# A sparse expert layer whose last tiles reach the residual by a one-hot product, and the two mixers behind it

## The chip, the cores and the metric

The kernel runs on one core of a Trainium2 chip, in one launch. The metric is the device time in microseconds (us) of that core; the time before is the median of three runs. A core has TensorE (PE in the rows; PEld is its weight load), VectorE (DVE), ScalarE (ACT), GpSimd (POOL) and SyncE (SP, which here issues most DMAs). All tensors are float32.

## The reference, cut to what matters

Two transformer-like blocks over 512 tokens of width 1024. The part around the change is the second half of each layer of the first block, a mixture of 16 experts of which each token takes two, and the mixer that follows it.

```python
x = x + g1 * mixer_i(rmsnorm(x, mix_norm[i]) * (1 + sc1) + sh1)     # layer 0: fox, layer 1: MLA
h = rmsnorm(x, ffn_norm[i]) * (1 + sc2) + sh2
# hier_moe: a group of 4 experts by softmax, 2 experts in the group, weights in `combine` (T x 16)
a = einsum('td,edf->tef', h, w_gate); u = einsum('td,edf->tef', h, w_up)      # d 1024, f 256
out = einsum('tef,efd->td', silu(a) * u * combine[..., None], w_down)
x = x + g2 * out                                   # g2: a row of 1024 from the conditioning
...
# second block, after layer 1: 16 meta rows ahead of the tokens (528), then
h = rmsnorm_2(concat(meta, x), norm_pre[0])
u = h @ w_in + b_in                                # 1024 -> 8192: x0, x1, v, z, 2048 channels each
y = bidir_long_conv(dwconv(v) * dwconv(x1), filters) * dwconv(x0) * silu(z)  # the hyena mixer
```

## The kernel before, in words

Tokens lie in four tiles of 128 rows (`NT`), and the residual `self.x` stays on the chip in four tiles of 128x1024. A float32 product is three matmuls (`mm3`, L147) of a rounded part and a rest: `split` (L121) makes the rounded part on ScalarE (L125) and the rest on VectorE (L128). `weights` (L136) loads a block of 512 KB into a `raw` buffer (L133, a ring of 8 in the expert phase) and splits it.

`moe(l)` sorts the tokens by expert into tables of 128 row numbers per expert (`tix` as integers, `tf` as floats, with the weights beside them) and goes over 16 experts. `front(e)` (L1174) gathers an expert's rows and computes its gate and up products (`expert_in`, L1021); `expert_out` (L1044) transposes the result, splits it, multiplies by the down weights into two PSUM banks (12 matmuls of 512 columns), has ScalarE copy these to `yo` (one buffer, L1060) and GpSimd add `yo` row by row to the array `yd` in DRAM (an indirect DMA, L1061). `front(e+1)` is issued ahead of `expert_out(e)`, so that down product e stands behind gate and up product e+1 on TensorE. Between them lie parts of the filters that the hyena mixer needs later (`hy_filter`, a generator: 32 parts a layer, of which 30 in layer 0 and 28 in layer 1 are spread over the loop).

An expert with more than 128 tokens leaves the rest to overflow tiles, numbered in `otab`. The weights of the first are loaded whether it exists or not, with the expert's number in a register (six blocks); `tc.If(n_any > 0)` (L1206) holds its work, and `tc.For_i(1, n_ov, 1)` (L1209) goes over further ones. With these inputs layer 0 has none and layer 1 has one: 16 scatters in layer 0 and 17 in layer 1, and neither layer goes round the loop. Behind it stand the last filter parts (two in layer 0, four in layer 1).

The next phase reads `yd` back (`moe_sum`, L1220 to L1222): four tiles of 512 KB by SyncE. `moe_norm` (L338) multiplies a tile by the gate row `g2` (L346, L359), adds it to the residual (L345), sums the squares (VectorE for tile 0, L354; ScalarE for others, L352), takes the root on GpSimd (L119), scales (L360), in layer 0 adds a shift (L362), and transposes the tile on TensorE (`put_T`, L374), a tile after the other.

In `mla` (L704) the projection 1024 to 672 follows, as two halves of 336 columns: `gemm_tok` does the first half of all four token tiles, then the second half of all (L774 copies the results), with the weights of the first half asked for between the reads of the sums. In `hyena` (L1389) the tokens of 528 columns are cut into two halves of 264, so that the first half needs token tiles 0 and 1 only; `streams(ct)` (L1465) computes the four projections of a channel tile one after the other, both halves each, and there are 16 channel tiles.

SyncE's queue, and each engine's order, are those in which the program issues its instructions.

Of the kernel before, what the change touches and what calls it, by code (L numbers as in the profile page):

```python
# [10 lines left out]
F32 = mybir.dt.float32  # L11
F32R = mybir.dt.float32r
BF16 = mybir.dt.bfloat16
I32 = mybir.dt.int32
# [58 lines left out]
class Model:  # L73
# [264 lines left out]
    def moe_norm(self, ys, gain, hT, c0, tags, shift=None):  # L338


        nc, ph = self.nc, self.ph
        V = nc.vector

        def add(t):
            return V.tensor_add(self.x[t], self.x[t], ys[t])  # L345
        V.tensor_mul(ys[0], ys[0], self.g2)  # L346
        add(0)
        for t in range(NT):
            x, h = self.x[t], ys[t]
            ss, r = [self.sm.tile([128, 1], F32, tag=n, name=n) for n in ("ss", "rstd")]  # L350
            if t:
                nc.scalar.activation(h, x, AF.Square, accum_out=ss)  # L352
            else:
                V.tensor_tensor_reduce(out=h, in0=x, in1=x, op0=ALU.mult, op1=ALU.add, scale=1.0, scalar=0.0, accum_out=ss)  # L354
            self.rsqrt(r, ss, 1.0 / D, EPS)
            if t < 2:
                self.midpow = self.lastpow
            if t < NT - 1:
                V.tensor_mul(ys[t + 1], ys[t + 1], self.g2)  # L359
            m = V.scalar_tensor_tensor(h, x, r, gain, op0=ALU.mult, op1=ALU.mult)  # L360
            if shift is not None:
                m = V.tensor_add(h, h, shift)  # L362
            if t < NT - 1:
                self.order(add(t + 1), m)
            self.put_T(h, hT, c0 + t * 128, tags)
            yield t
# [337 lines left out]
    def mla(self):  # L704
# [3 lines left out]
        with Phase(self, "mla", dict(mm=2, pv=1, sc=2, tq=2, tp=1), bufs,  # L708
# [7 lines left out]
            ys = [ph.t([128, D], F32, "qT", "y") for _ in range(NT)]  # L716
            sh, A = [ph.t([128, D], F32, "v", n) for n in ("sh", "A")]
            self.moe_sum(0, 0, ys[0])
            self.mod_to(A, 1, 1)
            self.mod_to(sh, 1, 0)  # L720
            self.moe_sum(0, 1, ys[1])
            raws = [self.raw(w_in(0)(0), 672)]
            self.moe_sum(0, 2, ys[2])
            raws.append(self.raw(w_in(0)(1), 672))
            self.moe_sum(0, 3, ys[3])
            raws.append(self.raw(w_in(0)(2), 672))
            h4 = four()
            for t in self.moe_norm(ys, A, h4, 0, ("tq", "tp"), sh):
                if t == 0:
                    pre = [self.weights(z, 672, keep=True) for z in raws + [w_in(0)(3)]]  # L730
            self.dump("xm0", self.x)
            hT = [[z[k // 4][:, k % 4, :] for k in range(KD)] for z in h4]
# [33 lines left out]
            ct = {}  # L766

            def evac_in(c):
                def f(t, p):
                    if c == 0:  # L770
                        if t % 2 == 0:
                            ct[t] = ph.t([128, 2, 672], F32, "PT", "ct")
                            ct[t], ct[t + 1] = ct[t][:, 0, :], ct[t][:, 1, :]
                    nc.scalar.copy(ct[t][:, c * 336:(c + 1) * 336], p)  # L774
                return f
            for c in range(2):
                self.gemm_tok(hT, KD, w_in(c), 336, evac_in(c), pre=None if c else pre)
# [266 lines left out]
    def expert_out(self, th, dn_w, idx, yd):  # L1044
# [19 lines left out]
    def moe(self, l):  # L1064
# [4 lines left out]
        with Phase(self, f"moe{l}", dict(dn=2, fl=2, mm=2, tp=2), bufs,  # L1069
# [109 lines left out]
            along, have = 32 - (2, 4)[l], 0  # L1179
            front(0)  # L1180
            for e in range(16):
# [8 lines left out]
                while have < (2 * e + 1) * along // 32:  # L1190
                    next(fil, None)
                    have += 1
                dw = lambda b: self.weights(dn[e, b], after=None if e else self.routed)
                self.expert_out(th.pop(e), dw, tix[:, e:e + 1], yd)
                while have < (2 * e + 2) * along // 32:
                    next(fil, None)
                    have += 1
            self.g2 = self.gate(l, 5)

            e = nc.values_load(otab[0:1, 0:1], min_val=0, max_val=15)  # L1200
# [5 lines left out]
            with tc.If(n_any > 0):  # L1206
                tv = self.expert_in(xg, lambda b: self.weights(wg[b]), tf[:, 16, 1:2])
                self.expert_out(tv, lambda b: self.weights(wd[b]), tix[:, 16:17], yd)
            with tc.For_i(1, n_ov, 1) as i:  # L1209
                e = nc.values_load(otab[0:1, ds(i, 1)], min_val=0, max_val=15)  # L1210
                ri = ph.t([128, 2], F32, "ri")
                nc.sync.dma_start(ri, tabd[:, ds(i + 16, 1), :].rearrange("p o n -> p (o n)"))
                rx = ph.t([128, 1], I32, "rx")
                V.tensor_copy(rx, ri[:, 0:1])
                tv = self.expert_in(gather(rx), lambda b: self.weights(dyn(gu, b, e)), ri[:, 1:2])
                self.expert_out(tv, lambda b: self.weights(dyn(dn, b, e)), rx, yd)
            for _ in fil:
                pass

# [897 lines left out]
```

## Time and profile before

| | us |
|---|---|
| median of three runs | 2632.34 |
| lowest and highest | 2628.58, 2633.38 |
| the profiled execution's own time | 2630.58 |
| its span, first to last instruction | 2628.8 |
| TensorE busy in the span | 2368.2 (90%) |
| VectorE busy | 1883.2 (72%) |
| ScalarE busy | 1484.7 (56%) |
| mean granted TensorE clock | 0.953 of full |

Times in the rows are counted from the span's start. A row of the order of time gives its start, its duration, the engine, the line and operation, what it writes and reads, and in brackets how long the engine had been idle before it and what ended that. The ends of matmuls are modelled, so the distance of two starts is a matmul's time in a row of them.

### The profile page before, as it was taken

To read this page: it belongs to the slowest core of one execution; us is meant where nothing else is said; L and a number is where in the kernel's file an instruction comes from. 1 tells how busy PE (TensorE), PEld (TensorE's weight loads), DVE (VectorE), ACT (ScalarE), POOL (GpSimd) and SP (SyncE) were. 2 spreads that over 40 slices of the span, in tenths; PEclk is the share of its full clock that TensorE was granted. 3 is DMA by queue.
4 is the path that set the end of the run, shared out by engine and by line. 5 is a ranking of instruction groups with operands and counts; after the bars stand their busy time and mean duration, and the time that the engine had idled before them with its cause. 6 is when DMAs were issued, how large, how long until landed. Compare 5 with 4: busy or idle time off the path is not lost.

```text
span 2628.8 us, 39566 instructions
## 1 busy us (share of the span) xinstructions
PE 2368.2 (90%) x14551; PEld 1956.1 (74%) x14551; DVE 1883.2 (72%) x4015; ACT 1484.7 (56%) x2902; POOL 258.4 (10%) x268
## 2 busy tenths in 40 slices
PE   6889977997899958895999999999799999999888
PEld 5667756775766746674999999997577777777666
DVE  7888877986688677785566666664657878777755
ACT  5575756885567356783444444443336666665652
POOL 1100113121122022211000000000100000000000
PEclk9899988998999979997999999999899999999989
DMA  7786659997211299995422222224322111112232
GB/s 260 245 256 201 225 165 299 338 314 227 74 34 49 84 287 297 304 289 169 130 94 91 90 90 90 90 68 135 117 96 69 41 73 60 70 52 69 90 108 80
DMA packets 130845, 389.07 MB, mean 148 GB/s; under 512 B 23290, under 2 KB 34794, under 8 KB 129880
## 3 DMA queue, kind: packets, MB, share of 16 engines
q1 hardware_dynamic: 115640, 330.31, 36.9%
q0 software_dynamic: 12704, 47.48, 7.4%
q10 hardware_dynamic: 2304, 8.72, 0.8%
q8 instruction: 116, 1.90, 0.3%
q14 instruction: 81, 0.66, 0.1%
HBM read 332.68 MB, written 53.77 MB: 147 GB/s over the span
## 4 chain that ended last, share of the span: by engine, by line
PE 44%; DVE 5%; ACT 2%; issue 2%; DMA 1%; POOL 0%; POOLq 0%; SPq 0%; ACTq 0%; DVEq 0%
PE ps_mm L150 10%; PE ps_mm L151 10%; PE ps_mm L152 10%; PE ps_sc L1781 1%; PE ps_b L152 1%; PE ps_b L150 1%; PE ps_b L151 1%; PE ps_sc L1782 1%; PE ps_tp L1811 1%; ACT whi L125 1%; PE ps_tl L1723 1%; PE ps_tp L1524 1%; PE ps_pv L150 1%; DVE wlo L128 1%; DMA yd<-yo,tix 1%
## 5 line engine op out<-in xcount | busy, mean ns | idle before, releaser
L128 DVE TENSOR_TENSOR wlo<-raw,whi 128x1024 fp32r<-128x1024 f32 (+3 forms) x426 | 499.9, 1185 | 236.5 <-ACT whi L125 228.6
L125 ACT CAST whi<-raw 128x1024 fp32r<-128x1024 f32 (+3 forms) x426 | 431.4, 1023 | 244.9 <-PE ps_mm L152 84.1
L150 PE MATMUL ps_mm<-hT,whi 128*128 128x264 f32 x1024 | 294.6, 288 | 0.9 <-ACT hT L125 0.8
L151 PE MATMUL ps_mm<-hT,whi 128*128 128x264 f32 x1024 | 293.3, 287 | 0.7 <-DVE hT L128 0.7
L152 PE MATMUL ps_mm<-hT,wlo 128*128 128x264 f32 x1024 | 291.8, 285 | 0.0
L150 PE MATMUL ps_mm<-whi,hT 128*128 128x512 f32 x512 | 206.4, 405 | 6.9 <-DVE zg L1716 5.9
L151 PE MATMUL ps_mm<-wlo,hT 128*128 128x512 f32 x512 | 205.5, 403 | 0.0
L152 PE MATMUL ps_mm<-whi,hT 128*128 128x512 f32 x512 | 205.1, 402 | 0.0
L151 PEld LDWEIGHTS ps_mm<-hT,whi 128*128 128x128 f32 x1024 | 194.7, 190 | 1.1 <-DVE hT L128 1.1
L150 PEld LDWEIGHTS ps_mm<-hT,whi 128*128 128x128 f32 x1024 | 193.9, 189 | 1.6 <-ACT hT L125 1.6
L152 PEld LDWEIGHTS ps_mm<-hT,wlo 128*128 128x128 f32 x1024 | 194.2, 190 | 0.0
L151 PE MATMUL ps_mm<-wlo,un 128*128 128x384 f32 (+1 forms) x376 | 141.2, 377 | 8.0 <-DVE wlo L128 7.7
L150 PE MATMUL ps_mm<-whi,un 128*128 128x384 f32 (+1 forms) x376 | 141.6, 380 | 4.7 <-ACT whi L125 1.6
L152 PE MATMUL ps_mm<-whi,un 128*128 128x384 f32 (+1 forms) x376 | 139.9, 377 | 0.0
L1789 ACT ACTIVATE P<-P,nm 128x528 f32<-128x528 f32 x128 | 94.3, 737 | 70.6 <-DVE P L1786 69.0
L1458 ACT ACTIVATE u<-ps_mm,hb 128x264 f32<-128x264 f32 x96 | 46.3, 482 | 137.5 <-PE ps_mm L152 137.5
L119 POOL TENSOR_TENSOR r<-rs,mhalf 128x4 f32<-128x4 f32 (+1 forms) x72 | 77.8, 1084 | 401.8 <-DVE rs L118 383.4
L150 PEld LDWEIGHTS ps_mm<-whi,hT 128*128 128x128 f32 x512 | 96.7, 189 | 27.3 <-DVE zg L1716 6.8
L150 PE MATMUL ps_mm<-whi,xgT 128*128 128x512 f32 x264 | 108.9, 413 | 7.0 <-ACT xgT L125 7.0
L219 DVE CUSTOM_DVE_ANT_0 ada<-ada,crow 128x1024 f32<-128x1024 f32 x80 | 97.6, 1220 | 19.5 <-DMA ada<-in_w_ada_dram 19.0
L152 PEld LDWEIGHTS ps_mm<-whi,hT 128*128 128x128 f32 x512 | 96.8, 189 | 18.1
L151 PEld LDWEIGHTS ps_mm<-wlo,hT 128*128 128x128 f32 x512 | 96.5, 189 | 17.5 <-issue 0.2
(586 smaller groups left out, 6310.2 us busy)
## 6 DMA issues: line engine op xcount, KB each, us to landing
raw<-in_moe_gu_dram SPq DMA_DIRECT2D x136, 512.0 KB, 7.5
ada<-in_w_ada_dram SPq DMA_DIRECT2D x96, 512.0 KB, 4.2
raw<-in_moe_dn_dram SPq DMA_DIRECT2D x68, 512.0 KB, 6.2
raw<-in_hy_w_dram SPq DMA_DIRECT2D x64, 512.0 KB, 3.5
raw<-in_da_w_dram SPq DMA_DIRECT2D x64, 512.0 KB, 4.9
raw<-in_fox_w_dram SPq DMA_DIRECT2D x32, 384.0 KB, 4.4
hs<-ht ACTq DMA_DIRECT2D x16, 532.0 KB, 7.3
H<-hs SPq DMA_DIRECT2D x16, 532.0 KB, 3.5
```

What stands on the lines that cost most here:

```text
L119: self.lastpow = nc.gpsimd.tensor_tensor(out, t, self.mhalf[:in_.shape[0]].to_broadcast(list(in_.shape)), op=ALU.pow)
L125: nc.scalar.copy(hi, src)
L128: return nc.vector.tensor_sub(lo, src, hi.bitcast(F32))
L150: r = nc.tensor.matmul(o, a[0], b[0], start=first, stop=False)
L151: nc.tensor.matmul(o, a[0], b[1], start=False, stop=False)
L152: self.lastmm = nc.tensor.matmul(o, a[1], b[0], start=False, stop=last)
L219: nc.vector.tensor_tensor_reduce(out=t, in0=t, in1=self.crow, op0=ALU.mult, op1=ALU.add, scale=1.0, scalar=0.0, accum_out=v[:, j:j + 1])
L1458: A.activation(u[:, 1 + hs.start:1 + hs.stop], p, AF.Identity, bias=hb[:, c:c + 1])
L1524: nc.tensor.transpose(p[:, cs], ab[:, f, cs], self.ident)
L1723: nc.tensor.matmul(tp[32 * j:32 * j + 16, 0:64], xt[:, k, :], w[:, c0 + j * 64:c0 + (j + 1) * 64], start=(k == 0), stop=(k == KD - 1))
L1781: nc.tensor.matmul(sc[:, hf, 0:264], qs[mp][:, ts], kk[mp][:, fs], start=True, stop=False)
L1789: nc.scalar.activation(P, P, AF.Exp, bias=nm_, scale=-1.0, accum_out=sum_)
```

## The change

The scatter stays for experts 0 to 14. For expert 15, for the overflow tile and for further tiles `expert_out` gets the row numbers as floats (`tok`): it compares a table 0 to 511 with them, which gives a 128x512 matrix with a one at each row's token, multiplies the down product by `g2` on the way out of PSUM, and multiplies the transposed one-hot matrix with it, in plain float32 and per token tile and half, with VectorE adding each product to the residual. The loop over further tiles stands under a second branch. `out(14)` now precedes `front(15)`; expert 15's down product comes last, after the branches. The sums of `yd` are read, gated and added to the residual in the expert phase, ahead of expert 15's down product, into buffers of the `raw` ring; the filter's remaining parts come after all that (one more is put in front by `fill(31)`).

`moe_norm` loses gate and residual; the gain is multiplied before the root is there, and the shift goes into one instruction with the scale. In `mla` all eight weight blocks are asked for and split ahead of the norm (those of the second half into buffers of the tag `qk`), and the projection goes by token tile, both halves of a tile together. In `hyena` the first channel tile does the first halves of all four projections after token tiles 0 and 1, then the rest of the norm, then the second halves.

```diff
-    def moe_norm(self, ys, gain, hT, c0, tags, shift=None):
+    def moe_norm(self, hs, junk, gain, hT, c0, tags, shift=None):
...
+        def begin(t):
+            ss, rs[t] = [self.sm.tile([128, 1], F32, tag=n, name=n) for n in ("ss", "rstd")]
+            nc.scalar.activation(junk(), self.x[t], AF.Square, accum_out=ss)
+            V.tensor_mul(hs[t], self.x[t], gain)
+            self.rsqrt(rs[t], ss, 1.0 / D, EPS)
             if t < 2:
                 self.midpow = self.lastpow
+        begin(0)
+        for t in range(NT):
+            h, r = hs[t], rs.pop(t)
+            if shift is None:
+                V.tensor_scalar(h, h, r, None, op0=ALU.mult)
+            else:
+                V.scalar_tensor_tensor(h, h, r, shift, op0=ALU.mult, op1=ALU.add)
             if t < NT - 1:
...
+                begin(t + 1)
             self.put_T(h, hT, c0 + t * 128, tags)
             yield t
...
+            ws = [[], []]
+            for b in range(4):
+                w = self.weights(w_in(0)(b), 672)
+                ws[0] += [[z[:, j * 336:(j + 1) * 336] for z in w] for j in range(2)]
+            for b in range(4):
+                raw = self.raw(w_in(1)(b), 672)
+                for j in range(2):
+                    w = [ph.t([128, 336], F32R, "qk", "w1") for _ in range(2)]
+                    self.split(*w, raw[:, j * 336:(j + 1) * 336])
+                    ws[1].append(w)
             h4 = four()
...
+            for t in self.moe_norm(hs, lambda: jk, A, h4, 0, ("tq", "tp"), sh):
+                for c in range(2):
+                    p = ph.bank("mm")[:, :336]
+                    for k in range(KD):
+                        self.mm3(p, [z[k][:, t * 128:t * 128 + 128] for z in hT], ws[c][k], k == 0, k == KD - 1)
+                    nc.scalar.copy(ct[t][:, c * 336:(c + 1) * 336], p)
...
-            for c in range(2):
-                self.gemm_tok(hT, KD, w_in(c), 336, evac_in(c), pre=None if c else pre)
...
-    def expert_out(self, th, dn_w, idx, yd):
+    def expert_out(self, th, dn_w, idx, yd, tok=None):
...
+        if tok is not None:
+            Q = ph.t([128, S], F32, "sel")
+            nc.vector.tensor_scalar(Q, self.iota512, tok, None, op0=ALU.is_equal)
+            for c in range(2):
+                cs = slice(c * 512, (c + 1) * 512)
+                nc.vector.tensor_mul(yo[:, cs], acc[c], self.g2[:, cs])
+            for t in range(NT):
+                for c in range(2):
+                    cs = slice(c * 512, (c + 1) * 512)
+                    p = ph.bank("mm")
+                    nc.tensor.matmul(p, Q[:, t * 128:(t + 1) * 128], yo[:, cs], start=True, stop=True)
+                    nc.vector.tensor_add(self.x[t][:, cs], self.x[t][:, cs], p)
+            return
...
             along, have = 32 - (2, 4)[l], 0
+            self.g2 = self.gate(l, 5)
+            self.iota512 = ph.t([128, S], F32, "iota512")
...
             front(0)
-            for e in range(16):
+            for e in range(15):
...
-                if e < 15:
+                if e < 14:
                     front(e + 1)
...
+                fill(2 * e + 1)
+                out(e)
+                fill(2 * e + 2)
+
+            front(15)
             e = nc.values_load(otab[0:1, 0:1], min_val=0, max_val=15)
...
             with tc.If(n_any > 0):
                 tv = self.expert_in(xg, lambda b: self.weights(wg[b]), tf[:, 16, 1:2])
-                self.expert_out(tv, lambda b: self.weights(wd[b]), tix[:, 16:17], yd)
-            with tc.For_i(1, n_ov, 1) as i:
...
+                self.expert_out(tv, lambda b: self.weights(wd[b]), None, None, tf[:, 16, 0:1])
+            with tc.If(n_ov > 1):
+                with tc.For_i(1, n_ov, 1) as i:
...
+                    self.expert_out(tv, lambda b: self.weights(dyn(dn, b, e)), None, None, ri[:, 0:1])
+            fill(31)
+            dw = [self.weights(dn[15, b]) for b in range(2)]
+            for t in range(NT):
+                y = ph.t([128, D], F32, "raw", "y")
+                nc.sync.dma_start(y, yd[t * 128:(t + 1) * 128, :])
+                V.tensor_mul(y, y, self.g2)
+                V.tensor_add(self.x[t], self.x[t], y)
+            self.expert_out(th.pop(15), lambda b: dw[b], None, None, tf[:, 15, 0:1])
             for _ in fil:
                 pass
...
+            def streams(ct, halves=False):
...
+                if halves:
+                    yield
+                    for i, g in enumerate(run):
+                        for _ in g:
+                            pass
+                        if i == 1:
+                            V.tensor_mul(uus[ct % 2][:, 0:T], x1, v)
...
-            streams(0)
+            next(norm)
+            begun = streams(0, True)
+            next(begun)
+            for _ in norm:
+                pass
...
+            for _ in begun:
+                pass
```

## Rows read from the trace of the kernel before

**Rows 1.** The page's first part: busy us (share of the span) xinstructions of each engine.

```profile
PE 2368.2 (90%) x14551; PEld 1956.1 (74%) x14551; DVE 1883.2 (72%) x4015; ACT 1484.7 (56%) x2902; POOL 258.4 (10%) x268
```

**Rows 2.** Stretches of layer 0's end: busy us per engine, clock, DMA share, GB/s.

```profile
645.00:650.00 5.00, 0.00 (x0) 0.00 (x0) 4.26 (x7) 0.75 (x1) 0.58 (x1) 0.72 1.03 371
```

**Rows 3.** The same view in layer 1.

```profile
1210.00:1215.00 5.00, 0.00 (x0) 0.00 (x0) 0.00 (x0) 0.00 (x0) 0.35 (x1) 0.54 0.67 107
```

**Rows 4.** GpSimd in order of time, layer 0: start, us, what [idle before <-releaser].

```profile
608.85 2.64 POOL L1061 DMA_INDIRECT yd<-yo,tix  x1 [2.74 <-ACT yo L1060]
...
631.12 1.56 POOL L1061 DMA_INDIRECT yd<-yo,tix  x1 [5.71 <-ACT yo L1060]
```

**Rows 5.** SyncE's waits from 600 to 720: in total, times, longest.

```profile
SPq L1209 <- DMA yd<-yo,tix: 16.1, 2, 8.2
```

**Rows 6.** SyncE in order of time: the first row sum of each layer.

```profile
638.20 0.35 SPq L1222 DMA_DIRECT2D y<-yd  x1
...
1215.65 0.34 SPq L1222 DMA_DIRECT2D y<-yd  x1
```

**Rows 7.** VectorE in order of time, layer 0, tile 0.

```profile
641.79 1.23 DVE L346 TENSOR_TENSOR y<-y,gate 128x1024 f32<-128x1024 f32 x1 [3.10 <-DMA y<-yd]
643.05 1.22 DVE L345 TENSOR_TENSOR x<-x,y 128x1024 f32<-128x1024 f32 x1
...
648.78 1.22 DVE L362 TENSOR_TENSOR y<-y,sh 128x1024 f32<-128x1024 f32 x1
```

**Rows 8.** TensorE in order of time, layer 0: last down product to projection's end.

```profile
629.59 0.63 PE L152 MATMUL ps_dn<-whi,hd 128*128 128x512 f32 x1
...
650.05 1.11 PE L374 MATMUL ps_tq<-ident,y 128*128 128x128 f32 x4 [5.91 <-DVE y L362]
...
653.10 0.65 PE L150 MATMUL ps_mm<-whi,h 128*128 128x336 f32 x1 [1.09 <-ACT h L125]
...
655.12 0.48 PE L152 MATMUL ps_mm<-whi,h 128*128 128x336 f32 x1
655.40 0.48 PE L150 MATMUL ps_mm<-whi,h 128*128 128x336 f32 x1
...
696.65 0.31 PE L150 MATMUL ps_mm<-whi,h 128*128 128x336 f32 x1
...
696.95 0.32 PE L152 MATMUL ps_mm<-whi,h 128*128 128x336 f32 x1
```

**Rows 9.** TensorE in order of time, layer 1: branch to the mixer's projection.

```profile
1192.32 1.08 PE L1029 MATMUL ps_tp<-ident,xg 128*128 128x128 f32 x8 [1.56 <-issue]
...
1207.27 0.39 PE L151 MATMUL ps_dn<-wlo,hd 128*128 128x512 f32 x1
1207.50 0.40 PE L152 MATMUL ps_dn<-whi,hd 128*128 128x512 f32 x1
...
1239.69 1.94 PE L374 MATMUL ps_tp<-ident,y 128*128 128x128 f32 x8 [8.18 <-DVE y L360]
1242.38 0.59 PE L150 MATMUL ps_mm<-hT,whi 128*128 128x264 f32 x1 [0.76 <-ACT hT L125]
...
1248.50 1.03 PE L374 MATMUL ps_tp<-ident,y 128*128 128x128 f32 x8
...
1255.25 0.81 PE L150 MATMUL ps_mm<-hT,whi 128*128 128x264 f32 x2
```

**Rows 10.** VectorE in order of time, layer 1: tile 0's residual.

```profile
1223.78 1.22 DVE L345 TENSOR_TENSOR x<-x,y 128x1024 f32<-128x1024 f32 x1
```

**Rows 11.** VectorE's groups by form: busy us, mean ns of one | idle before, releaser.

```profile
L681 DVE TENSOR_TENSOR x<-x,ps_mm 128x512 f32<-128x512 f32 x16 | 10.9, 683 | 2.0 <-PE ps_mm L152 2.0
...
L416 DVE TENSOR_SCALAR P<-P,rr 128x512 f32<-128x512 f32 x16 | 7.7, 481 | 0.1
...
L311 DVE TENSOR_SCALAR htok<-x,rstd 128x1024 f32<-128x1024 f32 x4 | 3.4, 839 | 2.2 <-POOL rstd L119 2.2
```

**Rows 12.** TensorE in order of time, MLA scores: two fp32 matmuls of 512 columns.

```profile
741.78 1.07 PE L874 MATMUL ps_sc<-qT 96*128 96x512 f32 x2
```

More of the change, by code (lines that the diff above doesn't have):

```diff
@@ L336, in meta_T @@
         nc.vector.tensor_mul(d, p, gcol[:, :, None].to_broadcast([128, KD, NM]))
-    def moe_norm(self, ys, gain, hT, c0, tags, shift=None):
+    def moe_norm(self, hs, junk, gain, hT, c0, tags, shift=None):
         nc, ph = self.nc, self.ph
         V = nc.vector
[L344 to L355, printed above, removed]
+        rs = {}
+        def begin(t):
[3 more added lines that the diff above has]
+            self.rsqrt(rs[t], ss, 1.0 / D, EPS)
             if t < 2:
                 self.midpow = self.lastpow
-            if t < NT - 1:
[L359 to L364, printed above, removed]
+        begin(0)
[5 more added lines that the diff above has]
+                V.scalar_tensor_tensor(h, h, r, shift, op0=ALU.mult, op1=ALU.add)
+            if t < NT - 1:
+                begin(t + 1)
             self.put_T(h, hT, c0 + t * 128, tags)
@@ L1179, in moe, with out, fill @@
             along, have = 32 - (2, 4)[l], 0
+            self.g2 = self.gate(l, 5)
+            self.iota512 = ph.t([128, S], F32, "iota512")
+            for t in range(NT):
+                V.tensor_scalar(self.iota512[:, t * 128:(t + 1) * 128], self.iota, 128.0 * t, None, op0=ALU.add)
+            def out(e, tok=None):
+                dw = lambda b: self.weights(dn[e, b], after=None if e else self.routed)
+                self.expert_out(th.pop(e), dw, tix[:, e:e + 1], yd, tok)
+            def fill(upto):
+                nonlocal have
+                while have < upto * along // 32:
+                    next(fil, None)
+                    have += 1
             front(0)
-            for e in range(16):
+            for e in range(15):
                 if e == 2:
@@ L1418, in hyena @@
             fk, ik = ph.t([73, 2, 128], F32R, "fk"), ph.t([82, 2, 128], F32R, "ik")
-            self.order(nc.gpsimd.memset(fk.bitcast(F32), 0.0), self.midpow)
-            self.order(nc.gpsimd.memset(ik.bitcast(F32), 0.0), self.midpow)
+            for z in (fk, ik):
+                self.order(nc.gpsimd.memset(z.bitcast(F32), 0.0), self.midpow)
             hb = ph.t([128, 64], F32, "hb")
@@ L1474, in use @@
                     A.activation(th[:, hs], p, AF.Tanh, bias=hbh[:, ct:ct + 1], scale=0.5)
-                proj(3, ct, use)
+                go(proj(3, ct, use))
+                if halves:
+                    yield
+                    for i, g in enumerate(run):
+                        for _ in g:
+                            pass
+                        if i == 1:
+                            V.tensor_mul(uus[ct % 2][:, 0:T], x1, v)
                 V.scalar_tensor_tensor(th, th, 1.0, zb, op0=ALU.add, op1=ALU.mult)
@@ L1540, in long_conv @@
                 nc.sync.dma_start(self.yh[ct], y)
-            streams(0)
+            next(norm)
+            begun = streams(0, True)
+            next(begun)
+            for _ in norm:
+                pass
+            self.dump("xm1", self.x)
+            for _ in begun:
+                pass
             for ct in range(CH):
@@ L1545, in hyena @@
                 if ct < CH - 1:
-                    streams(ct + 1)
+                    for _ in streams(ct + 1):
+                        pass
             if "yh" in self.dbg:
```

96 lines of the change are left out of this document (36 added, 60 removed).

## The prediction

> **What bounds the kernel now.** I read the engine totals first, then the span in stretches of 5 us, then the order of time on each engine at the two places that the diff touches, then the wait lists. TensorE is busy for 90% of the span [rows 1], so time can be had only where it stands still. Two such places are the ends of the expert loops: in layer 0 it does nothing from 645 to 650 [rows 2], in layer 1 nothing from 1210 to 1215 [rows 3]. The reader should see there that no other engine is full for long either; it is a chain. Layer 0: the last down product ends at 630.2, its copies feed a scatter issued at 631.12 [rows 4, 8], SyncE stands in the loop's entry until that scatter has landed [rows 5], the first row sum is read at 638.20 [rows 6], VectorE starts on it at 641.79 and is through with tile 0 at 650.0 [rows 7], TensorE transposes at 650.05 and begins the projection at 653.10 [rows 8]. The projection's 192 matmuls (4 tiles x 2 halves x 8 x 3) follow each other at 0.152 us at the full clock (two of them in 0.30, the last two rows of [rows 8]), so they are 29.2 us of work, but they end at 697.1: 44.0 us, 14.8 more, because all first halves go ahead of all second halves and each tile's norm is waited for. Layer 1 has an overflow tile, so its branch is taken: on TensorE from 1192.32 to 1207.9, then a scatter, first read at 1215.65, residual of tile 0 added at 1225.0, tile 1 transposed only at 1239.69, first projection matmul at 1242.38, and a second hole from the transposes at 1248.50 to 1255.25 [rows 6, 9, 10].
>
> **The change part by part.**
>
> *The scatter and the loop's entry.* Row sums no longer wait for expert 15 nor for the overflow tile, only for expert 14, whose down product now comes ahead of expert 15's gate and up products. With one buffer for the product, its copies wait for expert 13's scatter: issued at 608.85, landing in about 7.1 us (631.12 to 638.20 for the last one), so 616; two copies and the issue 1.5 (0.9 from 630.2 to 631.12, where the first copy was under way): scatter at 617.5, landed at 624.6. Layer 0's sums can be read 13.6 us earlier. Two skipped branches stand in place of the zero-trip loop. The trace shows no loop under a branch; the cheap end is 0, the dear end the 7.8 us that the loop's entry took in layer 1 (1207.9 to 1215.65, most of it the landing). The nearest row is TensorE's 1.56 us of "issue" at the entry of the taken branch [rows 9], which stays; for the second branch I take 1.
>
> *The one-hot product.* Per tile of 128 rows: one comparison of 128x512 (0.48), two products with the gate from PSUM (0.68 each), 8 fp32 matmuls of 512 columns, 8 adds from PSUM (0.68 each, 0.6 back to back) [rows 11]. Two fp32 matmuls of 96x512 took 1.07 us together [rows 12], so 0.54 each at the most: below the adds, so the adds set the pace. From the last down matmul: 0.7 + 0.5 + 8 x 0.68 = 6.6 us; the first pair, tile 0, is in after 2.5. Against it stand copy, scatter and landing: 7.8 us. So the product costs what it replaces; its gain is that tile 0 goes on alone. The Trainium skill's "FP8 and Floating Point Precision" (section TensorE Precision Notes) says that true fp32 is four passes through the array; with 0.23 for a pass of 512 columns a matmul here would be 0.92 by it, an estimate, and the matmuls would set the pace. The row's 0.54 lies nearer to two passes.
>
> *Row sums.* The four products with the gate and four adds (1.22 each) now all come ahead of the norm, 9.6 us of VectorE together, where only two came ahead of tile 0 before. Cover: expert 15's down product, its two weight splits and the branch. Without it all 9.6 are on the path. The reads take buffers of the overflow tile's weights, so none can start before those are freed: in layer 0 at the branch, in layer 1 inside it. The gate's load moves ahead of the expert loop, where nothing waits for it until the first gate product: nothing.
>
> *Layer 0 sum.* Reads from 624.6, first at VectorE after 3.6 (638.20 to 641.79): 628.2; 9.6 of row sums: 637.8; gate products 1.4, first pair 1.3: tile 0 complete at 640.5 against 644.3 [rows 7]. From there the old chain took 5.8 to the transposes; it loses the separate shift add (1.2) and shares VectorE with six more adds (3.6) and the gain product (1.2): 4.6 to 9.4, I take 6: 646.5. Projection 3.05 later, 649.5 against 653.1: -3.6. The projection then holds 29.2, plus 24 matmuls at the lower clock (0.28 apart, from 655.12 to 655.40) 3.1, plus three tiles' transposes 3.1 (1.03 each, [rows 9]): 35 against 44.0: -9. But eight weight loads now precede it on SyncE, behind expert 15's two, the four sums and the two modulation rows, and their buffers are freed only when the product's tile is; I give back 2.6. Layer 0: -10. Bounds: -16 (weights on time, norm unhindered) and 0 (tile 0 as late as before, weights pacing).
>
> *Layer 1 sum.* Before the branch TensorE loses expert 15's 12 down matmuls (0.23 apart, [rows 9]: 2.7) and two filter parts (28 to 26 of 32), some 2 us: branch at 1187.6. To the last down matmul 15.6 as before: 1203.2; product 6.6: 1209.8; second branch 1: 1210.8. VectorE then has 9.6 of row sums, two weight splits (a pass over 128x1024 like the sums, 1.22) 2.4, a small split 0.4, comparison 0.5, gate products 1.4, first pair 1.3 = 15.6: tile 0 complete at 1226.4, against 1225.0 [rows 10]. From there to tile 1's transposes it was 14.7 us; now VectorE has six adds 3.6, two gain products 2.4, two scalings of 0.84 [rows 11], tile 0's splits 1.3 = 9.0, and up to 6.9 us of filter work (what lay between 1215.65 and the gate product ahead of [rows 10]): 9 to 16, I take 12: 1238.4, so -1.3. The hole up to 1255.25 (6.9 us, with the transposes) is filled by the other streams' first halves: -6.9. Layer 1: -8. Bounds -15 (filter parts fit into the branch's idle time) and +2.
>
> Together -18. The profiled execution took 2630.6 us (span 2628.8); 2612.6. The median of the runs, 2632.3, is 1.7 above it: 2614.
>
> **The rivals.**
>
> *All packs.* The filter parts find idle VectorE time ahead of the branch (VectorE is idle at 1210 to 1215, [rows 3]) and the weights are there: -16 and -15, 2601. Against it: VectorE's order is fixed when the kernel is built, and row sums cannot go ahead of the branch.
>
> *VectorE takes the chain's place.* With the filter's last parts between row sums and norm, tile 0 is ready when it was before; left are the fuller projection and the filled hole, less the weights: -4 and -1, 2627. For it: layer 1's own list of 15.6 us reaches 1226.4 with no slack.
>
> *Slower: second-half weights behind the filter.* They go into buffers that lie first in the MLA phase, where the expert phase had its filter tables. These are free only when the last filter part has run; four parts are left in layer 0 instead of two. TensorE goes in order: tile 0's second half waits, and all tiles behind it. It decides from the point where the last filter part ends after 656 (649.5 plus 7 for tile 0's first half); every us later is lost, and from 666 layer 0 loses. At 673 it is +7, with +1 in layer 1: 2640. Against it: in the trace TensorE was through with two parts 5.9 us before 650.05 [rows 8].
>
> *Matmuls set the product's pace.* If an fp32 matmul takes four passes of 0.23, the 8 of a product take 0.92 each in place of the adds' 0.68: 1.9 a product at the full clock, and there are three products, one in layer 0 and two in layer 1; 4 to 6 us, since part lies beside row sums: 2619. [Rows 12] speak against it. The rule for it is the one named above.
>
> *The branch still waits.* That the loop's entry barrier is met although skipped would leave layer 1 as it is and take 4 off layer 0's gain: 2624; I count it with the second rival.
>
> **How the numbers follow.** Forecast 0.49, all packs 0.18, VectorE (with the branch) 0.17, matmul pace 0.08, slower 0.08. About 0.2%, 5.3 us, is what a measurement here can tell from no change: below 2627.1 is faster. The second rival's case stands at that edge and is split in half: faster 0.49 + 0.18 + 0.08 + 0.08 = 0.83, same 0.09, slower 0.08. The range takes the bounds: most of the first rival below, the second above: 2597 to 2632.
>
> **What would show it.** Right: no scatter after expert 14's; no barrier between the branch and the first read; 24 fp32 matmuls in three products, at the adds' pace; the projection of layer 0 from about 649 in 35 us without holes; in layer 1 four first halves in a row from about 1241, and no hole behind them. Wrong: VectorE full from the branch to tile 1's transposes in layer 1; TensorE waiting in layer 0 for second-half weights; a first read later than 630.

## The result: slower by 0.9%, where 0.7% faster was forecast

The changed kernel takes 2654.14 us (median of five runs, 2647.91 to 2662.49), the kernel before 2633.38 beside it: ratio 1.0088, 95% interval 1.0068 to 1.0107. The forecast of 2614 and its range up to 2632 are missed. The profiled execution of after took 2662.49 (span 2660.8) against 2630.58, so the traces differ by 32 us where the medians differ by 21; stretches of one trace are therefore read as to their place, and sizes are taken from the ratios, by which the loss is 0.88%, 23 us.

The span of seven profiled executions, from the first gather on and cut at events that all have (us; "gather" is a layer's first gather of an expert's rows, "gate" the first gate of the hyena mixer):

| | layer 0: gather to projection | projection | to layer 1's gather | to hyena's first matmul | to gate | gate to end |
|---|---|---|---|---|---|---|
| before | 257.9 | 44.0 | 245.9 | 299.3 | 38.2 | 1348.2 |
| after | 278.7 | 37.1 | 245.5 | 313.3 | 38.3 | 1350.9 |
| e8, mixers only | 256.1 | 39.7 | 242.6 | 302.3 | 39.9 | 1346.5 |
| e9, MLA only | 259.4 | 40.5 | 242.5 | 302.5 | 38.0 | 1348.4 |
| e10, front(15) as before | 271.6 | 36.0 | 243.9 | 304.1 | 36.8 | 1348.2 |
| e11, and filter ahead | 268.9 | 37.1 | 245.6 | 298.7 | 36.6 | 1347.1 |
| e13, overflow product only | 258.3 | 39.7 | 243.3 | 297.1 | 39.3 | 1349.6 |

The loss has two places: 20.8 us ahead of layer 0's projection, of which the projection gives 6.9 back, and 14.0 between layer 1's first gather and the hyena mixer. They are the two chains of the prediction, now longer; forecast were 10 and 8 us less.

TensorE still has 90% of the span, with 33 us more of it [rows 1]. The page's first part, after:

```profile
PE 2401.6 (90%) x14599; PEld 1972.0 (74%) x14599; DVE 1905.0 (72%) x4060; ACT 1482.5 (56%) x2904; POOL 254.1 (10%) x265
```

**Layer 0, before the branch.** ScalarE of after in order of time (start, us, what, [idle before <-releaser]; the same columns in all rows below):

```profile
616.61 0.58 ACT L1066 COPY yo<-ps_dn 128x512 f32<-128x512 f32 x1 [3.47 <-DMA yd<-yo,tix]
617.09 0.59 ACT L1376 COPY fT<-ps_fl 128x512 f32<-128x512 f32 x1
617.56 0.61 ACT L1066 COPY yo<-ps_dn 128x512 f32<-128x512 f32 x1
618.04 0.62 ACT L125 CAST xgT<-ps_tp 128x512 fp32r<-128x512 f32 x1
```

Expert 14's copies waited for expert 13's scatter to land. Behind them in ScalarE's order stood a filter copy and the rounding of expert 15's rows, without which TensorE could not begin expert 15. That filter copy also held 6.7 us of filter matmuls, which ran ahead of expert 15's (617.73 to 624.42; its gate and up products end at 629.9). In order of time, TensorE and then SyncE and VectorE of after:

```profile
617.73 1.25 PE L1385 MATMUL ps_fl<-ftab,fT 128*128 128x266 f32 x2 [2.77 <-ACT fT L1376]
...
636.45 0.66 PE L1042 MATMUL ps_tp<-ident,th 128*128 128x128 f32 x2 [4.43 <-PEq L1224]
...
653.24 9.83 PE L1062 MATMUL ps_mm<-yo,sel 128*128 128x512 f32 x16 [5.01 <-DVE yo L1057]
662.50 0.69 PE L1386 MATMUL ps_fl<-fsk,fk 73*128 73x266 f32 x1
...
673.37 1.11 PE L370 MATMUL ps_tq<-ident,h 128*128 128x128 f32 x4 [7.11 <-DVE h L358]
...
675.67 0.63 PE L150 MATMUL ps_mm<-whi,h 128*128 128x336 f32 x1
...
712.64 0.32 PE L152 MATMUL ps_mm<-w,h 128*128 128x336 f32 x1
```

```profile
605.00 28.23 SPq L133 DMA_DIRECT2D raw<-in_moe_dn_dram  x4
633.39 3.05 SPq L1237 DMA_DIRECT2D y<-yd  x4
663.14 0.32 SPq L278 DMA_DIRECT2D sh<-modd  x1
663.51 1.45 SPq L133 DMA_DIRECT2D raw<-in_mla_w_dram  x3
```

```profile
641.14 2.36 DVE L128 TENSOR_TENSOR wlo<-raw,whi 128x1024 fp32r<-128x1024 f32 x2
643.41 2.36 DVE L1238 TENSOR_TENSOR y<-y,gate 128x1024 f32<-128x1024 f32 x2
...
650.22 2.36 DVE L1239 TENSOR_TENSOR x<-x,y 128x1024 f32<-128x1024 f32 x2
652.49 1.29 DVE L1057 TENSOR_TENSOR yo<-ps_dn,gate 128x512 f32<-128x512 f32 x2
653.81 0.68 DVE L1263 TENSOR_TENSOR fk<-ps_fl,fk 9x512 fp32r<-9x512 f32 x1
655.35 0.69 DVE L1063 TENSOR_TENSOR x<-x,ps_mm 128x512 f32<-128x512 f32 x1 [0.85 <-PE ps_mm L1062]
657.05 0.69 DVE L1063 TENSOR_TENSOR x<-x,ps_mm 128x512 f32<-128x512 f32 x1 [1.02 <-PE ps_mm L1062]
...
663.10 0.69 DVE L1063 TENSOR_TENSOR x<-x,ps_mm 128x512 f32<-128x512 f32 x1 [0.17 <-PE ps_mm L1062]
...
668.50 0.15 DVE L118 TENSOR_SCALAR rs<-ss 128x1 f32<-128x1 f32 x1 [4.70 <-ACT junk L347]
```

No scatter and no landing stand at the end any more [rows 4, 5], but everything after expert 15's gate and up products is one chain through VectorE: its weight splits, eight row sum passes (643.41 to 652.5), gate products, adds. Before, two passes made tile 0 whole [rows 7]. Then the norm waits too. ScalarE of after:

```profile
663.23 0.57 ACT L1388 ACTIVATE ht<-ps_fl,fnd,finv 128x266 f32<-128x266 f32 x1 [16.21 <-PE ps_fl L1386]
...
667.32 1.06 ACT L347 ACTIVATE junk<-x 128x1024 f32<-128x1024 f32 x1 [0.54 <-ACT ht L1390]
```

Tile 0 is whole at 657.7; its squares are taken at 667.32, since the filter's last part stands ahead of the norm on ScalarE, and its matmuls behind the one-hot product on TensorE (662.50). An input of theirs, `fk`, had itself been held on VectorE behind the row sums and gate products (653.81).

**Layer 1** begins 15 us later (its first gather at 958.31 instead of 943.04) and shows the same. TensorE and ScalarE of after:

```profile
1203.34 1.04 PE L1022 MATMUL ps_tp<-ident,xg 128*128 128x128 f32 x8
...
1219.01 7.70 PE L1062 MATMUL ps_mm<-yo,sel 128*128 128x512 f32 x16
...
1267.29 1.97 PE L370 MATMUL ps_tp<-ident,h 128*128 128x128 f32 x8 [6.45 <-DVE h L356]
...
1271.61 0.81 PE L150 MATMUL ps_mm<-hT,whi 128*128 128x264 f32 x2 [0.67 <-ACT hT L125]
...
1282.32 0.39 PE L150 MATMUL ps_mm<-hT,whi 128*128 128x264 f32 x1 [2.27 <-ACT x L1476]
```

```profile
1261.76 1.06 ACT L347 ACTIVATE junk<-x 128x1024 bf16<-128x1024 f32 x1 [0.40 <-ACT ht L1390]
...
1280.38 1.04 ACT L125 CAST whi<-raw 128x1024 fp32r<-128x1024 f32 x1 [6.48 <-DMA raw<-in_hy_w_dram]
```

They answer to [rows 9]. The overflow tile's product takes 7.70; squares come at 1261.76, 13.5 us after tile 0 is whole (1248.2). The four first halves run one after the other, but ScalarE waits 6.48 us for the fourth's weights, the first one's copies out of PSUM stand behind that, and so TensorE stands 2.27 us ahead of the third (1282.32).

### The profile page after: what moved, and what is told of

It is laid out like the page before. It is cut to its first block, busy times and chain, and to the rows that moved or that the text cites. A ratio compares the mean times of both kernels' runs of the same rounds, so it can differ in the third digit from the quotient of the medians.

```text
span 2660.8 us, 39638 instructions
## 1 busy us (share of the span) xinstructions
PE 2401.6 (90%) x14599; PEld 1972.0 (74%) x14599; DVE 1905.0 (72%) x4060; ACT 1482.5 (56%) x2904; POOL 254.1 (10%) x265
## 4 chain that ended last, share of the span: by engine, by line
PE 43%; DVE 5%; ACT 3%; issue 1%; DMA 1%; POOL 0%; POOLq 0%; ACTq 0%; DVEq 0%
PE ps_mm L150 10%; PE ps_mm L151 10%; PE ps_mm L152 10%; PE ps_sc L1827 1%; PE ps_b L152 1%; PE ps_b L150 1%; PE ps_b L151 1%; PE ps_sc L1828 1%; PE ps_tp L1857 1%; ACT whi L125 1%; PE ps_tl L1769 1%; DVE wlo L128 1%; PE ps_tp L1562 1%; PE ps_pv L150 1%; PE ps_tq L1857 1%
## 5 line engine op out<-in xcount | busy, mean ns | idle before, releaser
L128 DVE TENSOR_TENSOR wlo<-raw,whi 128x1024 fp32r<-128x1024 f32 (+2 forms) x422 | 497.1, 1189 | 230.1 <-ACT whi L125 224.1
L125 ACT CAST whi<-raw 128x1024 fp32r<-128x1024 f32 (+2 forms) x422 | 427.7, 1025 | 236.0 <-PE ps_mm L152 82.4
L150 PE MATMUL ps_mm<-whi,xgT 128*128 128x512 f32 x264 | 110.2, 417 | 6.6 <-ACT xgT L125 6.5
L152 PE MATMUL ps_mm<-whi,xgT 128*128 128x512 f32 x264 | 108.7, 412 | 1.7 <-DVE xgT L128 1.6
```

The costliest lines, as they stand in the source:

```text
L125: nc.scalar.copy(hi, src)
L128: return nc.vector.tensor_sub(lo, src, hi.bitcast(F32))
L150: r = nc.tensor.matmul(o, a[0], b[0], start=first, stop=False)
L152: self.lastmm = nc.tensor.matmul(o, a[1], b[0], start=False, stop=last)
```

## The experiments

Ratios are to the kernel before beside the same runs, with their 95% interval.

### Each half of the change by itself: e1, e8, e9

e1 is the kernel before with both mixers' new orders; the norm and the experts' end are the old ones.

> The kernel before, its expert phase, its scatters, its loop entry and its norm kept, with the two mixers' new order alone: the MLA projection by token tile with both halves, the hyena's first channel tile with four first halves. If the loss sits in the changed end of the expert phase (my theory), this is faster than the kernel before: layer 0's projection takes some 37 us in place of 44 (in the changed kernel it took 37.1, from 675.67 to 712.8), layer 1 gains 0 to 7: 2619 to 2627 against 2633. If the mixers' new order is itself what costs (weights late, buffers late), it is slower than the kernel before: 2640 or more.

Measured: 2638.98, 1.0024 (1.0012 to 1.0035). The mixers alone do not gain, and the loss is in layer 1 (318.7 us from its first gather to the hyena's first matmul, before 299.3). VectorE of e1:

```profile
1243.37 0.17 DVE L1432 TENSOR_SCALAR hbh<-hb 128x16 f32<-128x16 f32 x1 [13.74 <-DMA hb<-in_hy_b_dram]
```

The hyena mixer's tables are loaded as soon as a given root is there. In e1 that was tile 0's; their loads shared the DMA engines with the mixer's weights (busy all the time from 1230 to 1240), and a load of 32 KB, asked for at 1231.59, landed so late that VectorE stood 13.74 us ahead of tile 1's norm. e8 asks for tile 1 ahead of the tables, so they wait for tile 1's root as before:

```diff
+            next(norm)
...
-            next(norm)
             begun = streams(0, True)
```

> The kernel before with the two mixers' new order alone, and the hyena's tables released after tile 1's root, as before the change, in place of tile 0's. In the run without that, the tables' loads were issued from 1223.97 ahead of the rest, a small load that VectorE waited for in front of tile 1's norm landed 13.7 us late, and the third and fourth weights of the hyena came at 1239.6 and 1245.2: from the last scatter to the first projection product 49.5 us against 33.6. If that is the cause, layer 1 is back at 34 or less, layer 0 keeps its 8: 2619 to 2626. If the four first halves cost by themselves, it stays near 2639.

Measured: 2628.77, 0.9988 (0.9976 to 1.0000). So that loss was e1's own (after's hole ahead of the hyena mixer has another cause, below). The edit moves the tables' loads (1227.96 instead of 1223.97) and also VectorE's work for tile 1; which of the two counts, no run separates. The small load is asked for at 1225.24 here and lands in 3.2 us. e9 takes the hyena order out as well and leaves MLA's projection by token tile:

> The kernel before with the MLA projection by token tile alone; expert phase, norm and hyena as before. From the runs' layer 0 (40 us of projection in place of 44, and 3 to 4 behind it): -8, 2625. If layer 0's gain was given back later in the run with both mixers (that is, if its loss in layer 1 was partly layer 0's), it is 2630 or more.

Measured: 2626.52, 0.9982 (0.9971 to 0.9993): faster than both kernels, than the one before by 0.18%, 4.7 us. The hyena order adds nothing to it: hyena's first matmul to the gate is 39.9 in e8 and 38.0 in e9. The hole behind the transposes [rows 9] is smaller in e8, but TensorE is busy for 34.8 us of that stretch, before for 32.8. Stretches of e8 (length, busy us of PE, PEld, DVE, ACT and POOL with instructions in brackets, then the granted clock, DMA share, GB/s):

```profile
1242.00:1252.00 10.00, 8.01 (x67) 7.77 (x66) 1.29 (x2) 4.71 (x10) 0.00 (x0) 1.00 0.83 273
1252.00:1262.00 10.00, 7.69 (x40) 7.27 (x41) 2.82 (x4) 1.86 (x4) 0.54 (x1) 0.66 0.18 54
```

The first ten had the full 2.4 GHz; in the next, with a wait of 4.3 us in them, the mean granted was 0.66, so part of them ran at 1.2 GHz, and 40 matmuls took as long as 67 had.

### The filter's place: e2, e6

Both run all the filter's remaining parts ahead of the branch; e2 also reckons the loop's share from all 32, so that 30 run in the loop.

```diff
+            for _ in fil:
+                pass
             e = nc.values_load(otab[0:1, 0:1], min_val=0, max_val=15)
...
-            fill(31)
...
-            for _ in fil:
-                pass
```

> The changed kernel with all filter parts ahead of the branch; none is left behind the one-hot product. Theory F (the last filter parts hold up the norm: ScalarE's first square starts 9.6 us after tile 0 is complete in layer 0, 657.7 to 667.3, and 13.5 us in layer 1, 1248.2 to 1261.8): both gaps go, and what was in them (3 parts and 5 parts, near 1.9 us of TensorE each) lies ahead of the branch: -5 and -6, 2643 against 2654. If the norm is held by the row sums and the product alone, nothing is gained and the moved parts cost: 2654 to 2662.

Measured: 2642.65, 1.0036 (1.0024 to 1.0049): 0.52% of the 0.88 are gone. The hole ahead of the hyena mixer goes (313.3 to 300.1), layer 0 keeps its 277.5: there the rounding of the spread put a part an expert earlier, and the third expert took 23.4 instead of 14.1 between two scatters. e6 leaves the spread alone:

> The changed kernel with the filter's last parts ahead of the branch, as in the run with the filter first, but the loop's share of parts as in the changed kernel. In that run layer 0's third expert took 23.4 us in place of 14.1, since the first part came an expert earlier; the gain at the ends of the layers was 13 in layer 0 and 15 in layer 1. If that stall is the whole difference, this one is 8 to 11 faster than it: 2632 to 2635. If the parts cost the loop their time wherever they stand, it is as there: 2642.

Measured: 2646.95, 1.0059 (1.0043 to 1.0074); expected was better than e2, so that is a miss, and its interval still meets after's. Layer 0 improved to 273.3, layer 1 only to 306.1; why it falls behind e2 there was not settled. With the filter gone, squares still don't lead to transposes in layer 0; VectorE of e6:

```profile
657.03 0.69 DVE L1063 TENSOR_TENSOR x<-x,ps_mm 128x512 f32<-128x512 f32 x1 [1.05 <-PE ps_mm L1062]
...
664.40 0.15 DVE L118 TENSOR_SCALAR rs<-ss 128x1 f32<-128x1 f32 x1
...
668.21 1.28 DVE L358 SCALAR_TENSOR_TENSOR h<-h,rstd,sh 128x1024 f32<-128x1024 f32 x1 [1.34 <-DMA sh<-modd]
```

Tile 0 is whole at 657.7, and what its root needs is done at 664.40, behind all eight adds, which the program issues first; then the shift row, asked for late, is waited for.

### The place of the sums: e3, e7

The block of four reads, gate products and adds goes ahead of the branches; in e7 on top of e6.

> The changed kernel with the four reads of the row sums, their products with the gate and their adds ahead of both branches. Theory S (row sums and the product stand one after the other on VectorE: sums 643.4 to 652.5 in layer 0, then the gate products): layer 0's expert 15 is through about 9 us earlier; in layer 1 the sums push the overflow tile's weight splits back and give it back: -9, 2645. If the filter's remaining parts set the norm's start anyway, the parts come earlier too only as far as the product does, and it is -3 at the most: 2651. Slower than the changed kernel would be the overflow tile pushed back by more than the sums cost behind it: 2658.

> The same, with the reads of the row sums, their gate products and adds ahead of the branches too. Theory S: with the parts gone from the norm's front, the sums (9.1 us of VectorE between the last down product and the product with the one-hot matrix) are what is left in the chain: layer 0 gains 6 to 9, layer 1 nothing (the sums push the overflow tile's weight splits back by what they save behind it): 2624 to 2628. If the sums were beside other waits anyway: as the run before this one, 2634.

Measured: e3 2649.07, 1.0067 (1.0049 to 1.0085); e7 2648.51, 1.0061 (1.0044 to 1.0078). Alone it gains about 5, about 3 in either layer, which is not clear of the noise; on top of e6 nothing. In e3 the squares still wait for the filter: tile 0 of layer 0 is whole at 653.0, squares start at 662.13. So moving the serial row sums is worth little by itself.

### The product's four passes: e4, e12

The product goes as two matmuls of a rounded part and a rest; the one-hot matrix is exact in the rounded type.

```diff
-                    nc.tensor.matmul(p, Q[:, t * 128:(t + 1) * 128], yo[:, cs], start=True, stop=True)
+                    for i in range(2):
+                        nc.tensor.matmul(p, Q[:, t * 128:(t + 1) * 128], ys[i][:, cs], start=i == 0, stop=i == 1)
```

> The changed kernel with the one-hot product as two fp32r matmuls of a rounded part and a rest instead of one fp32 matmul; for it two more copies and two more subtractions. Theory P (an fp32 matmul of 512 columns takes 0.93 us at the full clock and 1.7 at the lower, and so sets the product's pace in place of the adds): the three products (10.3 us in layer 0, 8.4 and 11 in layer 1) shrink to 8 adds at 0.6 to 0.7 and 1.5 for the split: -3 to -7, 2648 to 2651 against 2654. If the adds set the pace, it is the split's 1.5 us each on top: 2658.

Measured: 2656.93, 1.0085 (1.0068 to 1.0103), no gain; the two splits that it needs come ahead of it. VectorE of after, then of e4, in the overflow tile's product:

```profile
1220.17 0.69 DVE L1063 TENSOR_TENSOR x<-x,ps_mm 128x512 f32<-128x512 f32 x1 [0.52 <-PE ps_mm L1062]
...
1226.75 0.69 DVE L1063 TENSOR_TENSOR x<-x,ps_mm 128x512 f32<-128x512 f32 x1 [0.17 <-PE ps_mm L1062]
```

```profile
1219.15 1.28 DVE L1066 TENSOR_TENSOR x<-x,ps_mm 128x512 f32<-128x512 f32 x2
...
1225.26 0.69 DVE L1066 TENSOR_TENSOR x<-x,ps_mm 128x512 f32<-128x512 f32 x1 [0.18 <-PE ps_mm L1065]
```

The eight adds follow each other at 0.94 in after (6.58 for seven steps) and still at 0.87 in e4, with half the passes. But the clock is not the same. Stretches of the product, of after and then of e4 (columns as above):

```profile
1219.00:1223.00 4.00, 3.99 (x9) 1.45 (x10) 2.77 (x5) 0.00 (x0) 0.00 (x0) 1.00 0.00 0
```

```profile
1220.00:1222.00 2.00, 2.00 (x5) 1.19 (x6) 1.37 (x3) 0.00 (x0) 0.00 (x0) 0.62 0.00 0
1222.00:1223.50 1.50, 1.50 (x4) 0.59 (x3) 1.13 (x2) 0.00 (x0) 0.00 (x0) 0.50 0.00 0
```

With two passes the granted clock fell to 1.2 GHz within the product, and two passes at that level (about 1.0 for a product from 1220.49 to 1223.51) take as long as four at the full 2.4 GHz. e12, on top of e11 below:

> The run before this one with the one-hot product as two fp32r matmuls of a rounded part and a rest. Alone this gained nothing, since the norm stood behind the filter's parts anyway. Theory P: now the product is on the path (the norm's scaling of tile 0 starts after the last add, 664.4 in the run with the parts flushed, and the product took 8 to 10 us there): 2 to 4 us less in layer 0, as much in layer 1: 4 to 7 under the run before this one. If the split's 1.5 us eats it: the same or slower.

Measured: 2635.74 against e11's 2636.30, no gain again; here too the clock falls within the products (0.55 from 1206 to 1209.5). Where it is back (0.96 from 1209.5 to 1212.5), four adds take 3.04, 0.76 each. So the passes do set the pace of after's product; halving them gains nothing as long as the clock and the splits ahead give it back.

### The second branch: e5

The second branch and the loop under it are left out (no third tile is computed).

> The changed kernel without the loop over further tiles and the branch around it (further tiles are left out; these inputs have none). TensorE stood 4.43 us at that branch in layer 0 (632.0 to 636.45) and 0.3 in layer 1. If the price is this branch's, it goes: 2649 to 2651 against 2654. If it is the first branch, skipped in layer 0, it stays: 2654.

Measured: 2658.53, 1.0109 (1.0091 to 1.0127), no gain. TensorE, VectorE and ScalarE of e5 in layer 0:

```profile
627.89 0.41 PE L1042 MATMUL ps_tp<-ident,th 128*128 128x128 f32 x2 [0.82 <-DVE filt L1341]
```

```profile
647.65 0.69 DVE L1063 TENSOR_TENSOR x<-x,ps_mm 128x512 f32<-128x512 f32 x1 [0.17 <-PE ps_mm L1062]
```

```profile
661.87 1.06 ACT L347 ACTIVATE junk<-x 128x1024 f32<-128x1024 f32 x1 [0.48 <-ACT ht L1381]
```

The wait of 4.43 us is this branch's: without it 0.82 is left, the first row sum starts 4.6 us behind the first read instead of 10.0, and tile 0 is whole 255.2 us after the first gather, 5.6 earlier than in after. But the filter's part now lies behind the whole product, the squares start 13.5 us after tile 0 instead of 9.6, and in layer 1 21.5 instead of 13.5. What the branch cost, the wait for the filter takes.

### Expert 15's place: e10, e11

```diff
-                if e < 14:
+                if e < 15:
                     front(e + 1)
...
-            front(15)
```

> The changed kernel with one part undone: expert 15's gather, gate and up product ahead of expert 14's down product, as before the change. Theory Y: with one buffer for the product, expert 14's copies wait on ScalarE until expert 13's scatter has landed (616.6 in layer 0), expert 15's transposed rows stand behind them (618.0), so its gate and up product ran from 624.4 to 629.9, where before the change it ended at 614.6; the branch (632) and the reads (633.4) follow it. Undone, layer 0 gains 6 to 9 and layer 1 some 3: 2642 to 2645 against 2654. If the reads wait for the scatter's landing and the rest for the reads, it is -4: 2650.

Measured: 2642.48, 1.0055 (1.0036 to 1.0074): 0.33% of the 0.88. The row sums are asked for at 629.65 instead of 633.39; there they wait 2.2 us for expert 14's scatter, which is now later (622.07, in after 618.44). And layer 0's squares start at 653.92, as soon as tile 0 is whole: the filter part that held them in after is through at 645.1. e11 adds e6's edit:

> The same, with the filter's last parts ahead of the branch too. Theory F gave 7 alone (2647 against 2654); if F and Y are two steps of one chain, they add up: 2635 to 2638. If the parts now push the branch back by what they no longer cost behind it, it is 2642 to 2645.

Measured: 2636.30, 1.0020 (1.0009 to 1.0032): 0.68% of the 0.88, 18 us, go with two places in the order of issue. Left are 5 us, in spite of a projection that is 7 shorter, and layer 0 says where: 268.9 to the projection, against 257.9 before.

### The overflow tile's product alone: e13, e14

e13 is e9 with the one-hot product for the overflow tile and further ones only; all 16 experts are scattered and the sums added in the norm as before. The gate row is loaded ahead of the loop, as in after. e14 also puts the filter ahead of the branch.

> The kernel before with MLA's projection by token tile, and of the product only the overflow tile's (and further tiles', with the loop under a branch): all 16 experts are scattered, the row sums are read and added in the norm as before. If the last expert's own product is what keeps the change behind the old order, then layer 0 here is that of MLA by token tile alone (projection 259 us after the first gather, against 269 with the last expert's product and the other two faults taken out), and layer 1 gains, since expert 15's scatter lands beside the overflow tile's matmuls: product until 9 us after the overflow tile's last down matmul, and tile 0's row sum 2.5 us behind it instead of 16.5 us behind that matmul, -5; less up to 4 for the four filter parts that lie behind the product. 2621 to 2626, below 2626.5. If instead the product of any tile costs more than a scatter and its landing, layer 1 loses too: 2630 to 2634.

> The same with the filter's remaining parts (two in layer 0, four in layer 1) ahead of the branch. If they stand in the norm's way as in the changed kernel, 2 to 4 us below the run without: 2618 to 2623. But here the wait for expert 15's scatter may have covered them in layer 0: then layer 0 is 2 us later and the sum is about the same, 2621 to 2626.

Measured: e13 2622.39, 0.9967 (0.9956 to 0.9979), the lowest of all, though its interval meets e9's; e14 2624.37, 0.9974 (0.9964 to 0.9984), no better. Layer 0 is back at 258.3 with the scatter at its end. So layer 0's 11 us go with the last expert's product and what comes with it: e13 also has the row sums back in the norm and the old norm, and no run takes these apart. SyncE and VectorE of e13 in layer 1:

```profile
1206.49 0.33 SPq L1242 DMA_DIRECT2D y<-yd  x1
```

```profile
1205.56 0.69 DVE L1074 TENSOR_TENSOR x<-x,ps_mm 128x512 f32<-128x512 f32 x1 [0.36 <-PE ps_mm L1073]
1206.61 0.16 DVE L1355 SCALAR_TENSOR_TENSOR finv<-fab 128x1 f32<-128x1 f32 x1 [0.36 <-DVEq L1228]
...
1213.13 1.22 DVE L345 TENSOR_TENSOR x<-x,y 128x1024 f32<-128x1024 f32 x1
```

The last down matmul starts at 1197.34. The sum of tile 0 comes 15.8 us behind it, in e9 it was 16.7, in the kernel before 16.3 [rows 9, 10]: the product takes as long as scatter and landing did, and the same filter work follows. From the branch to the hyena mixer e13 takes 50.5 and e9 50.1. The 5.4 us that e13 gains on e9 from the gather to the hyena mixer lie ahead of the branch, in the expert loop. Why the loop is shorter (two of its steps by 2.3 and 1.6 us) no run tells; it may be where its loads fall, the gate row's among them.

## Why the prediction was wrong

**Scatter and copies.** Right up to 616: the copies waited for expert 13's landing, forecast 616, measured 616.61. The step that failed is what came next: "Layer 0's sums can be read 13.6 us earlier" counted the waiting copies as free, and did not ask what stands behind them on ScalarE. That was expert 15; the branch comes behind its gate and up products (629.9), and the reads, by the prediction's own words not to be had before the branch, came at 633.39, not 624.6. e10, which undoes this place, gains 0.33%, 9 us in both layers together (intervals of after and e10 meet at 1.007). In its layer 0 only 3.7 of the 8.8 us come back at the reads; the rest of its gain there is the filter part that no longer holds the squares.

**Row sums and tile 0.** "Tile 0 complete at 640.5" came at 657.7. Of the 17.2, 8.8 are the late reads; 6.4 lie between read and first row sum (10.0 instead of 3.6), behind the branch, a filter part and the weight splits; most of it goes with the second branch, put at 1 (e5: 4.6 instead of 10.0). 2.5 are the product's first pair, at a granted clock of 0.50. The sums' size was right (9.1 for 9.6), their cover was not: nothing hides them, as VectorE's order has the splits ahead of them and the gate products behind. That order is not the program's line by line, as the text ahead of the prediction has it: VectorE of after compares for expert 15 (636.13) and works on a filter part that the program issues behind the product (638.24) ahead of the row sums (643.41).

**From there to the transposes.** Forecast 6 (4.6 to 9.4), measured 15.6; this overlap is the second step that failed. The sum counted VectorE's work alone, but the norm of tile 0 is not alone: the filter's last part is ahead of it on ScalarE (e2, e6, e11), the root's input behind all adds on VectorE, and the shift row is asked for only when the phase's buffers come free. In e11, with the filter away, it is still 10.7, from 649.56 to the transposes at 660.27; that and 5.9 us of later completion make layer 0's 11.

**The product.** Forecast 6.6; in the overflow tile it took 9.2, from the first gate product (1218.26) to past the last add. That the matmuls set the pace was the fourth rival, and its mechanism is what the rows show. What misled was a count of rows: [rows 12] is one matmul, not two, since 8 of them appear as 16 here. The Trainium skill's "FP8 and Floating Point Precision" (section TensorE Precision Notes) has true fp32 as four passes; the 7.70 for eight matmuls, 0.96 each, agrees with the 0.92 estimated by it. Halving the passes did not help (e4: 9.7 for the same stretch), since the splits came on top and the clock fell.

**The projection.** Forecast 35 us, measured 37.1 (from 675.67); e9, where it alone is changed, took 40.5 and gained 4.7. This step was right to 2 us, and by itself it pays.

**Layer 1.** The branch came 4.3 us earlier by its distance from the first gather (245.0, before 249.3), as forecast (4.7). Tile 0's completion, counted from the first gather, was 6.6 later than forecast, as row sums and weight splits there had filter work between them, and the filter parts, for which up to 6.9 was allowed on VectorE, took ScalarE and TensorE as well: 13.5 to the squares. The hole of 6.9 was filled with first halves, but nothing was won by it: from the first matmul to the gate it is 38.3 against 38.2, with the wait for late weights (the 6.48 above) in the same stretch.

**The rivals.** "VectorE takes the chain's place" named the right engine and stopped at a gain of 5. "The branch still waits" was right in that the reads stand behind the branch, and one of the signs of being wrong, a first read later than 630, came true. The slower rival, second-half weights behind the filter, did not occur: the projection ran without a hole of that size. Its cause, the filter's rest in the wrong place, was right, but it hit the norm, not the weights. The chance for slower, 0.08, was too small for a change that lengthens the last chain of an in-order engine in both layers.

## What to carry to other kernels

When a wait is moved, read what is queued behind the waiting instruction on its own engine, and price that, not the wait. Here a scatter with 8 us of latency and hardly any engine time at the end of a phase was cheaper than 10 us of work on the engine that the next phase needs first. And a filler that ran in idle time must be placed again when the idle time moves.

## What the runs showed that was not expected

- A float32 matmul appears as two rows: 16 rows for 8 matmuls, 7.70 us at the full clock and 9.83 in layer 0, where the stretch began at a lower one.
- A skipped branch held TensorE for 4.43 us in layer 0 (row above), 7.4 in e10, and 0.30 in layer 1. Leaving it out (e5) brought 0.82 in layer 0, yet no gain in all. What sets its length was not settled.
- A load of 32 KB, asked for while table loads were under way, was waited for 13.74 us in e1 and landed in 3.2 in e8, where it went out ahead of them: 1.0024 against 0.9988.
